# A streaming encoder layer: statistics of the last tiles taken at an earlier product, and the last product ended by column halves

## The chip, the cores and the metric

The kernel runs on one core of a Trainium2 chip. The metric is device time in microseconds, the median of several runs. Engines are named as in the profile: PE is TensorE (matmuls; PEld its weight loads), DVE is VectorE, ACT ScalarE, POOL GpSimd, SP SyncE, which issues most of the DMAs.

## The reference

One layer of a hybrid encoder in float32: a prompt of 2048 tokens and 128 tokens of eight streams, 17 tiles of 128 tokens with 1024 features. What matters here is the end of the layer, for each tile:

```python
f, conv_rows = conv_ffn(h, conv_prev, w_up, w_conv, b_conv, w_down)   # ends in (...) @ w_down, 2816 -> 1024
y = layer_norm(DEEPNORM_ALPHA * h + f, ln2_g, ln2_b)

def layer_norm(x, g, b):
    mu = jnp.mean(xf, axis=-1, keepdims=True)
    var = jnp.mean(jnp.square(xf - mu), axis=-1, keepdims=True)
    y = (xf - mu) * lax.rsqrt(var + LN_EPS) * g + b
```

Before it come the input projection, an mLSTM, a sliding-window attention, the output projection, a first layer norm and the up projection with its convolution and gate. The change touches none of that.

## The kernel before

The 17 tiles go through the feed-forward part in three blocks (`FBLOCKS`); the last block is tiles 12, 13, 14, 15 and 16. The down projection (`f_downs`) is the last stage. Each block's pairs of tiles and halves of `w_down` are multiplied by a Strassen-like scheme of seven products, numbered 1 to 7. The last block takes them in the order 1, 2, 4, 6, 5, 7, 3 (`DLAST`), so that "the second product" is number 2, "the sixth product" is the one numbered 6 and "the last product" is number 3. A product sums over 11 groups of 128 rows of `w_down`, taken two at a time in six units (`DUNITS`, the last with one group). A unit needs its weights and its activations split into a high and a low part: ACT rounds to the high part (L218), DVE subtracts (L219); tiles `uw` are split weights, `fu` split activations. Each group and tile costs three matmuls of 512 columns, high by high, high by low and low by high (L2090). The sums lie in eight banks of PSUM, one per tile and product, with the profile's names `dps`, `fup` and `fht`.

In the last block `ta` is tile 12 or 13 (for the product's column `p` 0 or 1) or tile 16 (`p` 2), `tb` tile 14 or 15. When a product is complete, `after` empties its bank: DVE adds it into the row block `yacc` of the tile (`add`, L2119 for the first contribution with the residual scaled by alpha, L2121 for the others). Product 2 completes the first 512 features of tiles 12, 13 and 16, product 3 the second 512. With product 3 each of these tiles is finished by `norm_last`: statistics of the two halves (`bn_stats`, L1564), their aggregate (L1565), the variance plus eps (L1566), GpSimd's power for the reciprocal root (L1567), two scalings of 512 columns by mean and gain (L1550), two by root and bias (L1552), each of these followed by its store. The last product takes tile 16, then 13, then 12. For tile 12 alone, `last_tile`, the first half's statistics are taken when product 2 is complete (L2102).

PE runs its instructions in the order in which the program writes them (`manual_schedule`). The instructions of the other engines are ordered by the tile framework's scheduler from dependencies and priorities; `add` runs at high priority. `tc.issue_after(i)` puts the instructions that its block writes behind instruction `i` on that instruction's engine. The framework also adds the semaphore waits between engines.

Of the kernel before, what the change touches and what calls it, by code (L numbers as in the profile page):

```python
# [8 lines left out]
F32 = mybir.dt.float32  # L9
F32R = mybir.dt.float32r  # L10
AF = mybir.ActivationFunctionType
ALU = mybir.AluOpType
AX = mybir.AxisListType

P = 128
# [32 lines left out]
HT = 2 * P  # L48
FBLOCKS = [[0, 1, 2, 3, 4, 5], [6, 7, 8, 9, 10, 11], [12, 13, 14, 15, 16]]
# [156 lines left out]
class Prog:  # L206
# [1338 lines left out]
    def norm_last(self, y, g, bb, dst, st):  # L1545

        nc, V = self.nc, self.nc.vector
        mv, s = self.stats(y, st)
        for c in (slice(0, 512), slice(512, 1024)):
            V.scalar_tensor_tensor(y[:, c], y[:, c], mv[:, 0:1], g[:, c], op0=ALU.subtract, op1=ALU.mult)  # L1550
        for c in (slice(0, 512), slice(512, 1024)):
            V.scalar_tensor_tensor(y[:, c], y[:, c], s[:, 0:1], bb[:, c], op0=ALU.mult, op1=ALU.add)  # L1552
            nc.sync.dma_start(dst[:, c], y[:, c])

    def stats(self, y, st=None):
        nc = self.nc
        V = nc.vector
        half = st is not None
        if not half:
            st = self.wp.tile([P, 2, 6], F32, name="lst", tag="lst", bufs=2)  # L1560
        mv = self.wp.tile([P, 2], F32, name="lmv", tag="lmv", bufs=2)
        s = self.wp.tile([P, 2], F32, name="lsc", tag="lsc", bufs=2)
        for i in range(half, 2):
            V.bn_stats(st[:, i], y[:, i * 512:(i + 1) * 512])  # L1564
        V.bn_aggr(mv, st)  # L1565
        V.tensor_scalar_add(s[:, 1:2], mv[:, 1:2], EPS)  # L1566
        nc.gpsimd.tensor_tensor(s[:, 0:1], s[:, 1:2], self.mhalf[:, 0:1], op=ALU.pow)  # L1567
        return mv, s
# [494 lines left out]
    def f_downs(self):  # L2063
        nc, a = self.nc, self.a
        V, S = nc.vector, nc.scalar
        mm = nc.tensor.matmul
        ln2 = []
        self.in_down = True
        for n in sorted(n for n in self.dq if n <= self.nt):
            for l in self.dq.pop(n):  # L2070
                self.d_load(*l)
        x = [self.fup.tile([P, 512], F32, name="fht", tag="fht", bufs=2) for _ in range(2)]
        banks = self.banks[0] + self.banks[1] + x


        role = {1: (0, 1, 2), 2: (0, 1, 2), 4: (3, 5, 0), 7: (3, 5, 2), 6: (6, 7, 4), 5: (6, 7, 4), 3: (6, 7, 4)}
        nb, nu = len(FBLOCKS), len(DUNITS)
        ys, ops = {}, {}
        last_tile = FBLOCKS[-1][0]
        st = self.wp.tile([P, 2, 6], F32, name="st", tag="st", bufs=1)  # L2080

        def product(s, p, units):
            ps = banks[role[s][2 if p == np_ else p]]
            c = slice(p * P, p * P + P)
            for u in units:
                wh, wl, fh, fl = ops[u]
                n = len(DUNITS[u])
                for k in range(n):
                    for i, (l, r) in enumerate(((fh, wh), (fh, wl), (fl, wh))):
                        mm(ps, l[:, k, c], r[:, k], start=s in (1, 4, 7) and u == 0 and k == 0 and i == 0,  # L2090
                           stop=u == nu - 1 and k == n - 1 and i == 2, skip_group_check=True)

        def after(s, p):
            ps = banks[role[s][2 if p == np_ else p]]
            ta, tb = (tiles[2 * np_], None) if p == np_ else (tiles[p], tiles[np_ + p])
            if s == 1:
                with self.tc.high_priority():
                    S.copy(banks[role[6][2 if p == np_ else p]], ps)
            elif s == 2:
                add(ta, 0, ps, True)  # L2100
                if ta == last_tile:
                    V.bn_stats(st[:, 0], ys[ta][:, :512])  # L2102
            elif s in (4, 6):
                add(tb, 0, ps, s == 4)
            elif s == 5 and tb is not None:
                add(tb, 1, ps, True)
            elif s == 7:
                add(tb, 0, ps, False)
                add(tb, 1, ps, False)
                pending.append(finish(tb, b, s))  # L2110
            elif s == 3:
                add(ta, 1, ps, True)
                pending.append(finish(ta, b, s))

        def add(t, half, ps, first):
            y = ys[t][:, half * 512:half * 512 + 512]
            with self.tc.high_priority():
                if first:
                    V.scalar_tensor_tensor(y, y, ALPHA, ps, op0=ALU.mult, op1=ALU.add)  # L2119
                else:  # L2120
                    V.tensor_add(y, y, ps)  # L2121

        def finish(t, b, step):
            if b == nb - 1 and step == 3:
                self.norm_last(ys[t], *ln2, a["y"][t], st if t == last_tile else None)
                return
            y, (g, bb) = ys[t], ln2
            mv, sc = self.stats(y)
            yield
            V.scalar_tensor_tensor(y, y, mv[:, 0:1], g, op0=ALU.subtract, op1=ALU.mult)  # L2130
            yield
            V.scalar_tensor_tensor(y, y, sc[:, 0:1], bb, op0=ALU.mult, op1=ALU.add)
            (nc.sync if b == nb - 1 else nc.gpsimd).dma_start(a["y"][t], y)

        pending = []

        def step():
            for f in pending[:2]:
                if next(f, self) is self:
                    pending.remove(f)  # L2140

        for g, (b, s, u) in enumerate(self.dseq):
            tiles = FBLOCKS[b]
            h, one = self.d_shape(b)
            np_ = h // P
            ts = [*tiles[:np_], *tiles[2 * np_:]] if s == 1 else tiles[np_:2 * np_] if s == 2 else []
            if 0 <= u - 2 < len(ts):
                t = ts[u - 2]
                ys[t] = self.f3.tile([P, D], F32, name="yacc", tag="yacc", bufs=6)
                nc.sync.dma_start(ys[t], self.zh[t])  # L2150
            if g == 3 * nu:
                for n in ("ln2_g", "ln2_b"):
                    t = self.fp.tile([P, D], F32, name="f_" + n, tag="hst", bufs=2)
                    nc.sync.dma_start(t, a[n].to_broadcast([P, D]))
                    ln2.append(t)
            ops[u] = *self.dw.pop((b, s, u)), *self.df.pop((b, s, u))
            if g == 0:
                for bank in x:
                    mm(bank, ops[0][2][:, 0, :P], ops[0][0][:, 0], start=True, stop=True, skip_group_check=True)
            cols = [*range(np_), *([np_] if one and s in (1, 2, 5, 3) else [])]  # L2160
            last = b == nb - 1 and s == DLAST[-1]
            if not last:
                for p in cols[::-1] if s == 7 else cols:
                    product(s, p, [u])
            elif u == 0:
                cols = cols[::-1]
                for p in cols:
                    product(s, p, [u])
            elif u == nu - 1:

                cols = cols[::-1]
                for p in cols:
                    product(s, p, range(1, nu))
                    after(s, p)
                    for _ in pending.pop():
                        pass

            if b < nb - 1:
                step()
            if u == nu - 1 and not last:  # L2180
                for p in cols[::-1] if s == 7 else cols:
                    after(s, p)
            while self.nw < min(g + 5, len(self.dseq)):
                self.d_weights()
            while self.nt < min(g + 6, len(self.dseq)):
                self.d_tokens()
            if b == nb - 1 and self.nw != len(self.dseq) - 1:
                with self.tc.issue_after(self.low):
                    step()
        while pending:  # L2190
            step()
# [15 lines left out]
```

## Time and profile before

| | us |
|---|---|
| median of 3 runs | 2295.34 (2293.25 to 2296.85) |
| the profiled execution | 2293.86 |
| its span, first to last instruction | 2292.1 |
| PE busy | 2273.5 |
| DVE busy | 1809.8 |
| ACT busy | 1272.4 |
| POOL busy | 278.7 |
| granted TensorE clock, mean | 0.999 |

A row of the timeline has the start, the time, the engine, the line, the operation, what it writes and reads, the shape, how many instructions are merged, and in brackets the engine's idle time before it and what ended that. A row of a group has the number of instructions behind the x, then their busy time and the mean of one in nanoseconds, then the idle time before them. A row of the waits has the waiting engine and what it waited for, the total, how often and the longest. The chain is followed back from the last instruction; the pieces of it are given in order of time.

### The profile page before, as it was taken

How to read it: one execution, taken by the hardware profiler on the slowest of the kernel's cores; microseconds unless marked ns; L12 is line 12 of the kernel's file. 1: busy time of each engine (PE TensorE's matmuls, PEld its weight loads, DVE VectorE, ACT ScalarE, POOL GpSimd, SP SyncE). 2: the span in 40 equal slices, each digit the busy share in tenths (PEclk: the TensorE clock that was granted, in tenths of full speed). 3: DMA queues.
4: the chain of work that ended last, by engine and by line, in shares of the span. 5: the costliest groups of instructions: out<-in, count | busy, mean ns of one | idle time of the engine just before them, and what ended most of it. 6: DMA issues, size and time to landing. Idle time of an engine off the chain costs nothing.

```text
span 2292.1 us, 39775 instructions
## 1 busy us (share of the span) xinstructions
PE 2273.5 (99%) x14293; PEld 2090.7 (91%) x14293; DVE 1809.8 (79%) x3068; ACT 1272.4 (56%) x2373; POOL 278.7 (12%) x509
## 2 busy tenths in 40 slices
PE   8999999999999999999999999999999999999998
PEld 8999999999878778999999999999999988888876
DVE  8777687777788879998778777778766786895987
ACT  5453476776766656555556555555555644444442
POOL 0001001000121110211112000013111200200200
PEclk9999999999999999999999999999999999999999
DMA  8989998898998867898778999988998786757752
GB/s 283 323 305 322 316 315 276 273 313 297 333 317 263 278 219 262 314 328 299 282 269 271 302 303 306 312 265 288 324 290 264 255 292 216 254 169 224 252 157 85
DMA packets 302133, 631.30 MB, mean 275 GB/s; under 512 B 47404, under 2 KB 140656, under 8 KB 301936
## 3 DMA queue, kind: packets, MB, share of 16 engines
q1 hardware_dynamic: 297264, 615.06, 79.2%
q0 software_dynamic: 3520, 10.56, 1.5%
q10 hardware_dynamic: 1152, 3.15, 0.4%
q8 instruction: 113, 1.85, 0.3%
q14 instruction: 84, 0.69, 0.1%
HBM read 457.02 MB, written 171.64 MB: 274 GB/s over the span
## 4 chain that ended last, share of the span: by engine, by line
PE 83%; DVE 3%; issue 1%; ACT 1%; DMA 1%; POOL 0%; SPq 0%; DVEq 0%; ACTq 0%; POOLq 0%
PE dps L1882 20%; PE fup L1882 20%; PE dps L713 8%; PE fup L2090 7%; PE dps L2090 7%; PE fht L2090 6%; PE dps L223 3%; PE dps L225 2%; PE dps L224 2%; PE ppo L1359 1%; PE ppt L1353 1%; PE psc L1314 1%; PE fht L1706 1%; PE pcu L1231 1%; PE dps L739 1%
## 5 line engine op out<-in xcount | busy, mean ns | idle before, releaser
L1882 PE MATMUL fup<-hh,uw 128*128 128x384 f32 (+1 forms) x1848 | 478.2, 328 | 0.0
L1882 PE MATMUL dps<-hh,uw 128*128 128x384 f32 (+1 forms) x1848 | 478.0, 328 | 0.0
L1882 PEld LDWEIGHTS fup<-hh,uw 128*128 128x128 f32 x1848 | 330.2, 188 | 0.0
L1882 PEld LDWEIGHTS dps<-hh,uw 128*128 128x128 f32 x1848 | 330.1, 188 | 0.0
L1882 PE MATMUL fup<-hl,uw 128*128 128x384 f32 (+1 forms) x924 | 302.9, 328 | 1.0 <-DVE hl L219 1.0
L1882 PE MATMUL dps<-hl,uw 128*128 128x384 f32 (+1 forms) x924 | 302.7, 328 | 0.0
L1940 DVE SCALAR_TENSOR_TENSOR cc<-u,cw,cc 128x768 f32<-128x768 f32 (+1 forms) x264 | 258.0, 978 | 39.3 <-ACT cc L1938 30.8
L713 PE MATMUL dps<-w,oh 128*128 128x256 f32 x1344 | 254.8, 285 | 0.1
L218 ACT CAST uw<-wraw 128x1024 fp32r<-128x1024 f32 x126 | 123.3, 978 | 228.2 <-PE dps L2090 122.2
L219 DVE TENSOR_TENSOR w<-wraw,w 128x1024 fp32r<-128x1024 f32 (+2 forms) x163 | 186.0, 1149 | 61.6 <-ACT w L218 58.6
L218 ACT CAST w<-wraw 128x1024 fp32r<-128x1024 f32 (+2 forms) x163 | 160.2, 992 | 113.8 <-PE dps L713 53.7
L713 PEld LDWEIGHTS dps<-w,oh 128*128 128x128 f32 x1344 | 210.9, 188 | 11.2 <-issue 8.1
L219 DVE TENSOR_TENSOR uw<-wraw,uw 128x1024 fp32r<-128x1024 f32 x126 | 142.2, 1129 | 61.2 <-ACT uw L218 61.2
L713 PE MATMUL dps<-w,ol 128*128 128x256 f32 x672 | 188.2, 280 | 0.0
L1882 PEld LDWEIGHTS fup<-hl,uw 128*128 128x128 f32 x924 | 173.7, 188 | 1.7 <-DVE hl L219 1.6
L1882 PEld LDWEIGHTS dps<-hl,uw 128*128 128x128 f32 x924 | 173.7, 188 | 0.0
L2090 PE MATMUL fup<-uw,fu 128*128 128x512 f32 x726 | 173.6, 396 | 0.0
L713 PE MATMUL dps<-oh,w 128*128 128x256 f32 x896 | 168.0, 283 | 3.9 <-DVE w L219 2.2
L2090 PEld LDWEIGHTS fup<-uw,fu 128*128 128x128 f32 x726 | 136.5, 188 | 32.7
L2090 PE MATMUL dps<-uw,fu 128*128 128x512 f32 x660 | 164.8, 396 | 0.0
L2090 PEld LDWEIGHTS dps<-uw,fu 128*128 128x128 f32 x660 | 124.1, 188 | 29.8
L713 PEld LDWEIGHTS dps<-oh,w 128*128 128x128 f32 x896 | 140.0, 188 | 10.1 <-issue 4.1
(320 smaller groups left out, 4567.6 us busy)
## 6 DMA issues: line engine op xcount, KB each, us to landing
uw<-zw SPq DMA_DIRECT2D x176, 512.0 KB, 5.0
zw<-uw SPq DMA_DIRECT2D x88, 512.0 KB, 3.3
w<-zws SPq DMA_DIRECT2D x72, 512.0 KB, 6.0
wv<-wup SPq DMA_DIRECT2D x66, 512.0 KB, 5.2
wraw<-wi SPq DMA_DIRECT2D x65, 512.0 KB, 5.2
wraw<-zt SPq DMA_DIRECT2D x60, 512.0 KB, 4.3
wraw<-wdn SPq DMA_DIRECT2D x45, 512.0 KB, 4.9
wraw<-wo SPq DMA_DIRECT2D x40, 512.0 KB, 5.1
```

The costliest lines, as they stand in the source:

```text
L218: nc.scalar.copy(hi, src)
L219: return nc.vector.tensor_sub(lo, src, hi.bitcast(F32)).ins
L223: mm(out, ah, bh, start=start, stop=False)
L224: mm(out, ah, bl, start=False, stop=False)
L225: mm(out, al, bh, start=False, stop=stop)
L713: mm(o, l, r, start=s in (1, 7) and c == k == i == 0, stop=k == 3 and i == 2, skip_group_check=True)
L739: mm(o, x, w, start=k == i == 0, stop=k == KD - 1 and i == 2, skip_group_check=True)
L1231: nc.tensor.matmul(ps[:, i], kw[:, h], v1[:, h], start=True, stop=True)
L1314: nc.tensor.matmul(ps[kvh][:, j, :nk], q[rs, j0 + j], k[rs, sel], start=i == 0, stop=i == 2)
L1882: mm(ps, l[:, k], r[:, k], start=s in (1, 7) and k == 0 and i == 0, stop=k == 3 and i == 2, skip_group_check=True)
L1940: V.scalar_tensor_tensor(c[:, v], u[:, i:i + n], w[i], c[:, v], op0=ALU.mult, op1=ALU.add)
L2090: mm(ps, l[:, k, c], r[:, k], start=s in (1, 4, 7) and u == 0 and k == 0 and i == 0, stop=u == nu - 1 and k == n - 1 and i == 2, skip_grou ...
```

## The change

Tiles 16, 13 and 12 each get a tag of their own for statistics, and when product 2 is complete all three have the statistics of their first half taken. Tile 12's are taken in two groups of 256 columns, so that its tile holds four groups. In the last product tiles 16 and 13 are done as before, with the statistics of their second half alone left to do. Tile 12's part of the product is written in two steps: units 1 to 3 over all 512 columns, then units 4 and 5 (three groups) over columns 0 to 255, then the same units over columns 256 to 511. After each half its add and its statistics follow, put behind tile 13's last scaling on DVE.

```diff
     def norm_last(self, y, g, bb, dst, st):
-        mv, s = self.stats(y, st)
+        mv, s = self.stats(y, st, True)
...
-            V.scalar_tensor_tensor(y[:, c], y[:, c], s[:, 0:1], bb[:, c], op0=ALU.mult, op1=ALU.add)
+            last = V.scalar_tensor_tensor(y[:, c], y[:, c], s[:, 0:1], bb[:, c], op0=ALU.mult, op1=ALU.add).ins
             nc.sync.dma_start(dst[:, c], y[:, c])
+        return last
+
+    def stat(self, st, y, half, *parts):
+        n = st.shape[1] // 2
+        w = 512 // n
+        for i in parts or range(n):
+            c = half * 512 + i * w
+            self.nc.vector.bn_stats(st[:, half * n + i], y[:, c:c + w])
...
-        for i in range(half, 2):
+        for i in range(2 if whole else half, 2):
             V.bn_stats(st[:, i], y[:, i * 512:(i + 1) * 512])
...
-        st = self.wp.tile([P, 2, 6], F32, name="st", tag="st", bufs=1)
+        early = (FBLOCKS[-1][-1], *FBLOCKS[-1][1::-1])
+        sts = {t: self.wp.tile([P, 4 if t == last_tile else 2, 6], F32, name="st", tag=f"st{i}", bufs=1) for i, t in enumerate(early)}
-        def product(s, p, units):
-            ps = banks[role[s][2 if p == np_ else p]]
+        def product(s, p, units, m=slice(0, 512)):
+            ps = banks[role[s][2 if p == np_ else p]][:, m]
...
-                        mm(ps, l[:, k, c], r[:, k], start=...)
+                        mm(ps, l[:, k, c], r[:, k, m], start=...)
...
                 add(ta, 0, ps, True)
-                if ta == last_tile:
-                    V.bn_stats(st[:, 0], ys[ta][:, :512])
+                if ta in sts:
+                    self.stat(sts[ta], ys[ta], 0)
...
-        def add(t, half, ps, first):
-            y = ys[t][:, half * 512:half * 512 + 512]
+        def add(t, half, ps, first, c=slice(0, 512)):
+            y, ps = ys[t][:, half * 512:half * 512 + 512][:, c], ps[:, c]
...
             if b == nb - 1 and step == 3:
-                self.norm_last(ys[t], *ln2, a["y"][t], st if t == last_tile else None)
+                if t != last_tile:
+                    self.stat(sts[t], ys[t], 1)
+                behind.append(self.norm_last(ys[t], *ln2, a["y"][t], sts[t]))
                 return
...
-                for p in cols:
+                for p in cols[:-1]:
                     product(s, p, range(1, nu))
                     after(s, p)
                     for _ in pending.pop():
                         pass
+                p = cols[-1]
+                product(s, p, range(1, nu - 2))
+                for i in range(2):
+                    m = slice(i * HT, i * HT + HT)
+                    product(s, p, range(nu - 2, nu), m)
+                    with self.tc.issue_after(behind[-1]):
+                        add(tiles[p], 1, banks[role[s][p]], True, m)
+                        self.stat(sts[tiles[p]], ys[tiles[p]], 1, i)
+                for _ in finish(tiles[p], b, s):
+                    pass
```

The built programs show what moves. The order on PE at the end of the program, with the semaphores that an instruction waits for; before (`fht` with x54 is tile 13's 27 matmuls and tile 12's 27):

```order
L2090 MATMUL dps<-uw,fu 128x512 x4
L2090 MATMUL dps<-uw,fu 128x512 [waits Activation_49]
L2090 MATMUL dps<-uw,fu 128x512 [waits DVE_49]
L2090 MATMUL dps<-uw,fu 128x512
L2090 MATMUL fht<-uw,fu 128x512 x54
```

and now:

```order
L2100 MATMUL dps<-uw,fu 128x512 [waits DVE_49]
L2100 MATMUL dps<-uw,fu 128x512
L2100 MATMUL fht<-uw,fu 128x512 x45
L2100 MATMUL fht<-uw,fu 128x256 x9
L2100 MATMUL fht<-uw,fu 128x256 [waits DVE_49]
L2100 MATMUL fht<-uw,fu 128x256 x8
```

Nine matmuls of tile 12 became eighteen of half the width, and the first of the second nine waits for DVE; the value it waits for is that of the add of columns 0 to 255, which is the second row of the piece of DVE after the change, below.

The order on DVE at the end of the program, from tile 13's scalings on; before (`lst` and `st` are statistics, `lmv` their aggregate, `lsc` the root's input and result):

```order
L1550 TENSOR_SCALAR yacc<-yacc,lmv,f_ln_g 128x512 x2
L1552 TENSOR_SCALAR yacc<-yacc,lsc,f_ln_b 128x512
L2119 TENSOR_SCALAR yacc<-yacc,fht 128x512
L1552 TENSOR_SCALAR yacc<-yacc,lsc,f_ln_b 128x512
L1564 BN_STATS st<-yacc 128x6
L1565 BN_AGGR lmv<-st 128x2
L1566 TENSOR_SCALAR lsc<-lmv 128x1
L1550 TENSOR_SCALAR yacc<-yacc,lmv,f_ln_g 128x512 x2
L1552 TENSOR_SCALAR yacc<-yacc,lsc,f_ln_b 128x512 x2
```

and now, from tile 13's last two scalings on:

```order
L1552 TENSOR_SCALAR yacc<-yacc,lsc,f_ln_b 128x512 x2
L2129 TENSOR_SCALAR yacc<-yacc,fht 128x256
L1562 BN_STATS st<-yacc 128x6
L2129 TENSOR_SCALAR yacc<-yacc,fht 128x256
L1562 BN_STATS st<-yacc 128x6
L1574 BN_AGGR lmv<-st 128x2
L1575 TENSOR_SCALAR lsc<-lmv 128x1
L1550 TENSOR_SCALAR yacc<-yacc,lmv,f_ln_g 128x512 x2
L1552 TENSOR_SCALAR yacc<-yacc,lsc,f_ln_b 128x512 x2
```

Both of tile 13's last scalings now stand ahead of tile 12's first add, and tile 12's add and statistics are two of each, in turn.

The order on DVE around the end of the sixth product, whose two adds (L2121, now L2131) empty the banks `fht` that the next product writes; before:

```order
L2121 TENSOR_TENSOR yacc<-yacc,fht 128x512
L219 TENSOR_TENSOR uw<-wraw,uw 128x1024
L2121 TENSOR_TENSOR yacc<-yacc,fht 128x512
L219 TENSOR_TENSOR fu<-r_23866,fu 128x2x256
L219 TENSOR_TENSOR fu<-r_23399,fu 128x2x128
```

and now:

```order
L219 TENSOR_TENSOR fu<-r_23868,fu 128x2x256
L219 TENSOR_TENSOR fu<-r_23401,fu 128x2x128
L2131 TENSOR_TENSOR yacc<-yacc,fht 128x512 x2
L219 TENSOR_TENSOR uw<-wraw,uw 128x1024
L219 TENSOR_TENSOR fu<-r_23868,fu 128x2x256
```

The weight split that stood between the two adds now stands behind both. At the end of the second product four BN_STATS rows stand where one stood (tile 12's two, and one each of tiles 13 and 16), and a subtraction of 256 columns (L2058, now L2067) moved from ahead of the sixth product's adds to behind them. The order on POOL and SP is unchanged, and that on ACT but for one activation split that moved by a unit.

More of the change, by code (lines that the diff above doesn't have):

```diff
@@ L1551, in norm_last, with stats @@
         for c in (slice(0, 512), slice(512, 1024)):
-            V.scalar_tensor_tensor(y[:, c], y[:, c], s[:, 0:1], bb[:, c], op0=ALU.mult, op1=ALU.add)
+            last = V.scalar_tensor_tensor(y[:, c], y[:, c], s[:, 0:1], bb[:, c], op0=ALU.mult, op1=ALU.add).ins
             nc.sync.dma_start(dst[:, c], y[:, c])
-    def stats(self, y, st=None):
+        return last
[5 more added lines that the diff above has]
+            self.nc.vector.bn_stats(st[:, half * n + i], y[:, c:c + w])
+    def stats(self, y, st=None, whole=False):
         nc = self.nc
@@ L2089, in product @@
                     for i, (l, r) in enumerate(((fh, wh), (fh, wl), (fl, wh))):
-                        mm(ps, l[:, k, c], r[:, k], start=s in (1, 4, 7) and u == 0 and k == 0 and i == 0,
+                        mm(ps, l[:, k, c], r[:, k, m], start=s in (1, 4, 7) and u == 0 and k == 0 and i == 0,
                            stop=u == nu - 1 and k == n - 1 and i == 2, skip_group_check=True)
@@ L2133, in finish @@
             (nc.sync if b == nb - 1 else nc.gpsimd).dma_start(a["y"][t], y)
-        pending = []
+        pending, behind = [], []
         def step():
```

## The prediction

> **What bounds the kernel now.** I read the page's busy times first, then TensorE's own waits, then the chain of work that ended last, and last the timeline of the two places where the programs differ. The busy times, the first and the last of the ten rows of TensorE's (PE's) waits, and the last piece of PE in the chain:
>
> ```profile
> PE 2273.5 (99%) x14293; PEld 2090.7 (91%) x14293; DVE 1809.8 (79%) x3068; ACT 1272.4 (56%) x2373; POOL 278.7 (12%) x509
> ```
>
> ```profile
> PE dps L713 <- DVE w L219: 2.2, 2, 1.4
> ...
> PE fht L2090 <- DVE yacc L2121: 0.2, 1, 0.2
> ```
>
> ```profile
> 2271.16 12.57 PE fht L2090 x54
> ```
>
> PE is busy for 99% of the span, and none of its waits names a DMA. So time can be won or lost in two ways only: PE is stopped somewhere, or the tail behind the last matmul changes. PE ends at 2271.16 + 12.57 = 2283.73, the span at 2292.1. What VectorE (DVE) does around that end:
>
> ```profile
> 2274.64 1.87 DVE L1564 BATCH_NORM_STATS2 lst<-yacc 128x6 f32<-128x512 f32 x3
> ...
> 2277.47 0.69 DVE L2119 SCALAR_TENSOR_TENSOR yacc<-yacc,fht 128x512 f32<-128x512 f32 x1
> 2278.08 0.74 DVE L1550 SCALAR_TENSOR_TENSOR yacc<-yacc,lmv,f_ln_g 128x512 f32<-128x512 f32 x1
> 2278.74 1.41 DVE L1552 SCALAR_TENSOR_TENSOR yacc<-yacc,lsc,f_ln_b 128x512 f32<-128x512 f32 x2
> 2280.07 0.68 DVE L1564 BATCH_NORM_STATS2 lst<-yacc 128x6 f32<-128x512 f32 x1
> 2280.78 0.21 DVE L1565 BATCH_NORM_AGGREGATE lmv<-lst 128x2 f32<-128x12 f32 x1
> 2281.03 0.15 DVE L1566 TENSOR_SCALAR lsc<-lmv 128x1 f32<-128x1 f32 x1
> 2281.10 1.41 DVE L1550 SCALAR_TENSOR_TENSOR yacc<-yacc,lmv,f_ln_g 128x512 f32<-128x512 f32 x2
> 2282.42 0.75 DVE L1552 SCALAR_TENSOR_TENSOR yacc<-yacc,lsc,f_ln_b 128x512 f32<-128x512 f32 x1
> 2283.75 0.69 DVE L2119 SCALAR_TENSOR_TENSOR yacc<-yacc,fht 128x512 f32<-128x512 f32 x1 [0.59 <-PE fht L2090]
> 2284.36 0.75 DVE L1552 SCALAR_TENSOR_TENSOR yacc<-yacc,lsc,f_ln_b 128x512 f32<-128x512 f32 x1
> 2285.02 0.69 DVE L1564 BATCH_NORM_STATS2 st<-yacc 128x6 f32<-128x512 f32 x1
> 2285.74 0.21 DVE L1565 BATCH_NORM_AGGREGATE lmv<-st 128x2 f32<-128x12 f32 x1
> ```
>
> After its last matmul DVE adds tile 12's product into the rows (2283.75), does one scaling that belongs to tile 13 (2284.36), then tile 12's statistics (2285.02) and their aggregate (2285.74). From the aggregate on both programs run the same instructions and the same last store. So the tail's change is the change in the moment at which tile 12's aggregate starts. The whole edit works on a few microseconds; 0.2% of 2295.34 is 4.6 us, about what a measurement of this kernel can tell from no change.
>
> **The change in the tail.** From start to start these rows give: an add 0.61 (2277.47 to 2278.08), two scalings 1.33 (2278.74 to 2280.07), statistics to their aggregate 0.71, aggregate to L1566 0.25, L1566 to the scaling 0.07. Of the three statistics at 2274.64 two go away, the first halves of tiles 16 and 13. In its new order DVE runs: tile 16's statistics 2274.64, aggregate 2275.35, scalings 2275.67 to 2277.00; tile 13's add as PE finishes it (27 of the 54 matmuls at 12.57/54 = 0.233), at 2277.47 as before; tile 16's last two scalings from 2278.08; tile 13's statistics 2279.41, aggregate 2280.12, L1566 2280.37, first two scalings 2280.44 to 2281.77. The last two wait for GpSimd's power:
>
> ```profile
> 2281.32 0.92 POOL L1567 TENSOR_TENSOR lsc<-lsc,mhalf 128x1 f32<-128x1 f32 x1 [3.46 <-DVE lsc L1566]
> ```
>
> It ends 1.21 behind the start of L1566 (2281.03 to 2282.24), now at 2281.58, in time. DVE is through with tile 13 at 2283.10.
>
> Now PE. Tile 12's last 27 matmuls become 18 of 512 columns, 9 of 256 on the left half of the bank and 9 of 256 on the right half. An early stage has 256 columns, and two DVE groups of the run's last 100 us show what width costs there:
>
> ```profile
> 60.27 0.39 PE L713 MATMUL dps<-oh,w 128*128 128x256 f32 x2
> ...
> 64.69 0.39 PE L713 MATMUL dps<-oh,w 128*128 128x256 f32 x2
> ```
>
> ```profile
> L219 DVE TENSOR_TENSOR fu<-r,fu 128x512 fp32r<-128x512 f32 x16 | 10.9, 683 | 0.0
> L219 DVE TENSOR_TENSOR fu<-r,fu 128x256 fp32r<-128x256 f32 x9 | 3.8, 418 | 0.1
> ```
>
> From 60.27 to 64.69 start 39 matmuls of 256 columns: 0.113 each, so two of them (0.227) cost no more than one of 512 (0.233), and the nine added instructions are free. The left half is done at 2277.44 + 18 x 0.233 + 9 x 0.113 = 2282.65. Its add, though, is queued behind tile 13's last scaling, so it runs at 2283.10. And PE's second group of nine waits for DVE in the new order: for that add, which reads the same bank. The trace has one such wait:
>
> ```profile
> 2220.87 0.69 DVE L2121 TENSOR_TENSOR yacc<-yacc,fht 128x512 f32<-128x512 f32 x1 [0.20 <-PE fht L2090]
> 2221.47 1.22 DVE L219 TENSOR_TENSOR uw<-wraw,uw 128x1024 fp32r<-128x1024 f32 x1
> 2222.61 0.68 DVE L2121 TENSOR_TENSOR yacc<-yacc,fht 128x512 f32<-128x512 f32 x1
> ```
>
> ```profile
> 2221.70 3.32 PE L2090 MATMUL fht<-uw,fu 128*128 128x512 f32 x12 [0.17 <-DVE yacc L2121]
> ```
>
> PE stood until the add on its bank was over (2220.87 + 0.69 = 2221.56) and began 0.14 later. The Trainium skill, "PSUM — Partial Sum Buffer", section "PSUM bank collisions raise a hardware error", says that TensorE writing and VectorE reading one bank collide even at different columns, and are to be kept apart by bank. By that rule the right half cannot overlap the add, and the row at 2221.70 agrees; were columns enough, the time would be the first rival's.
>
> A 256-wide add of this kind is not in the trace. By the two L219 rows 256 columns less save 0.265, so I take 0.42 for the add (0.69 less that) and 0.41 for the statistics, being nearest to these rows; the bounds are half the 512 row (0.34) and all of it (0.69). Then: left add 2283.10 to 2283.52; PE again at 2283.66; nine matmuls 1.02, and the last drains 0.28 in place of 0.11 (0.39 for a pair less 0.11), so 2284.85; right add 2284.87 to 2285.29; its statistics to 2285.72; aggregate at 2285.74, where it was. The tail's sum is 0.0. With the bounds for two adds and one statistics it runs from -0.2 to +0.8. The four-group aggregate in place of the two-group one I count as nothing (0.21 now, so at most 0.2 more). Without the halves, the early statistics alone would give 2283.75 + 0.69 + 0.02 + 0.69 + 0.02 = 2285.17, or -0.6: they gain, and the halves with their wait give it back.
>
> **The change at the second and sixth products.** After the second product's adds DVE gets four statistics for one: two of 512 columns more, and for tile 12 two of 256 in place of one of 512.
>
> ```profile
> 2191.53 0.68 DVE L2102 BATCH_NORM_STATS2 st<-yacc 128x6 f32<-128x512 f32 x1
> 2192.14 1.21 DVE L219 TENSOR_TENSOR uw<-wraw,uw 128x1024 fp32r<-128x1024 f32 x1
> ```
>
> ```profile
> 2190.61 15.54 PE L2090 MATMUL dps<-uw,fu 128*128 128x512 f32 x66
> ```
>
> One costs 0.61 (2191.53 to 2192.14); the increase is 2 x 0.61 + 0.05 = 1.27 us of DVE. The weight split behind it (2192.14 to 2193.35) is the fourth unit's of the product that PE begins at 2190.61, and PE needs it 36 matmuls later, at 2199.0. That cover of 5.6 us hides the 1.27; without it PE would wait 1.27.
>
> The scheduler also shifts DVE's rows up to the end of the sixth product. The chain there, and DVE's wait before the first add:
>
> ```profile
> 2221.70 1.64 PE fht L2090 x6
> ...
> 2223.34 1.68 PE fht L2090 x6
> ```
>
> ```profile
> DVE uw L219 <- ACT uw L218: 1.0, 2, 0.6
> ```
>
> Before, a weight split (2221.47) stands between the two adds, and PE's second six matmuls, whose bank the second add empties, start at 2223.34 and not 6 x 0.233 = 1.40 behind the first: 0.24 lost. Now the adds stand together, the second is over at 2222.25, and the 0.24 goes. Against it DVE reaches the first add with 1.27 more work, less a 256-wide subtraction moved behind (0.33), so 0.94; its idle time until there is 1.0 and 0.20 (the row at 2220.87), which holds that. With that cover gone PE would start 0.94 later. I take -0.2, with bounds -0.24 and +0.7.
>
> **Sum.** 0.0 - 0.2 = -0.2 us. The profiled execution took 2293.86 (its span 2292.1, 1.8 around it), so 2293.7 there. The median of the runs shown, 2295.34, lies 1.5 above it, so 2295.1. Both terms' bounds: -0.4 to +1.5.
>
> **The rivals.** First: the halves overlap, and PE doesn't wait for the left add. PE then ends at 2283.73 as before, DVE does the left add and its statistics from 2283.10 to 2283.95 and the right ones by 2284.83: the aggregate 0.9 earlier, with the other term 2294.2. For it speaks that the columns are disjoint, against it the wait in the order. Chance 0.10.
>
> Second: the pause costs more. The 256-wide steps cost nearly what 512 do, and DVE comes late to the sixth product's adds: +0.8 and +0.7, 2296.8. For it: the cover before the first add is thin (1.2 over 0.94); against it the 418 ns. Chance 0.18.
>
> Third, on the other side by more than 0.2%: two more tags for statistics lengthen a pool that was opened early, and in the built program the tiles of later pools on that side lie 160 bytes further in SBUF. About 169 MB of the kernel's transfers touch them. The queue's row, and the longest wait of a feeding engine for a DMA:
>
> ```profile
> q1 hardware_dynamic: 297264, 615.06, 79.2%
> ACT uw L218 <- DMA wv<-wup: 11.6, 5, 3.5
> ```
>
> If those transfers took 5% longer, that is 169/615 x 79.2% x 2292 x 5% = 25 us of queue time over the whole run. It decides where an engine that feeds PE already waits for a transfer; if a fifth reached PE, +5 us, 2300.3. Against it: PE's waits name no DMA, and a fifth of the queue's time is free. Chance 0.07. The Trainium skill, "DMA: Bandwidth & Descriptors", section "How a descriptor splits into AXI transactions", has a reason for it: a descriptor that starts off a 256-byte boundary fetches beats it does not use, by my estimate 5 on 128 for a 4 KiB row starting 160 bytes in. No run here shows it.
>
> The same shift could help instead, by as much: 2290.1, chance 0.05.
>
> **How the numbers follow.** My forecast has 0.60. Within 0.2% lie it and the first two rivals, 0.60 + 0.10 + 0.18 = 0.88; slower 0.07, faster 0.05. The likeliest gives 2295.1. The range goes from the first rival's 1.1 under the lowest run shown (2293.25, so 2292.1) to the upper bound over the highest (2296.85 + 1.5, so 2298.3) and leaves out the last two cases.
>
> **What would show it.** Right: a gap of about 1.0 us on PE before its last nine matmuls, ended by a 256-wide add at about 2283.1; tile 12's aggregate within 0.3 of 2285.74; the two adds of the sixth product side by side and one gap on PE there, not two. Wrong: no gap in the last product (first rival); 256-wide rows of 0.6, or PE stopped for over 0.5 at 2220 (second); DMA rows among PE's waits (third); or a span off by over 2 us with the tail as it was.

## The result, and the profile after

The changed kernel takes 2300.24 us (median of 10 runs, 2298.58 to 2301.26), beside 2294.02 (2293.01 to 2296.85) for the kernel before on the same chip: ratio 1.0025, 95% interval 1.0017 to 1.0033. It is slower by 0.25%, clear of noise, and lies above the predicted range. Its profiled execution took 2299.33 us, its span is 2297.6, 5.5 more than before.

The places that the change edits look as forecast. DVE's last rows in the timeline of the changed kernel, then PE's:

```profile
2287.09 1.41 DVE L1552 SCALAR_TENSOR_TENSOR yacc<-yacc,lsc,f_ln_b 128x512 f32<-128x512 f32 x2
2288.41 0.42 DVE L2129 SCALAR_TENSOR_TENSOR yacc<-yacc,fht 128x256 f32<-128x256 f32 x1
2288.86 0.43 DVE L1562 BATCH_NORM_STATS2 st<-yacc 128x6 f32<-128x256 f32 x1
2290.24 0.42 DVE L2129 SCALAR_TENSOR_TENSOR yacc<-yacc,fht 128x256 f32<-128x256 f32 x1 [0.95 <-PE fht L2100]
2290.70 0.43 DVE L1562 BATCH_NORM_STATS2 st<-yacc 128x6 f32<-128x256 f32 x1
2291.16 0.26 DVE L1574 BATCH_NORM_AGGREGATE lmv<-st 128x2 f32<-128x24 f32 x1
```

```profile
2276.30 11.73 PE L2100 MATMUL fht<-uw,fu 128*128 128x512 f32 x54
2288.89 1.32 PE L2100 MATMUL fht<-uw,fu 128*128 128x256 f32 x9 [0.86 <-DVE yacc L2129]
```

The row of 54 merges 45 matmuls of 512 columns and the first nine of 256; then PE stands 0.86 until the 256-wide add on its bank (2288.41 + 0.42 = 2288.83) is over. But everything comes 5.3 us late: the last product's group starts at 2276.30. In the timeline of the kernel before, the same group:

```profile
2270.99 12.72 PE L2090 MATMUL fht<-uw,fu 128*128 128x512 f32 x54
```

So 2276.30 - 2270.99 = 5.31 of the 5.5 us were lost before the tail. The page's busy times of the changed kernel, and its queue row:

```profile
PE 2279.9 (99%) x14302; PEld 2096.2 (91%) x14302; DVE 1810.0 (79%) x3071; ACT 1273.2 (55%) x2373; POOL 277.3 (12%) x509
```

```profile
q1 hardware_dynamic: 297264, 615.06, 79.4%
```

PE is busy 6.4 us longer with nine instructions more, and its waits, first and last two rows, name no DMA:

```profile
PE dps L713 <- DVE w L219: 2.1, 2, 1.3
...
PE pht L1187 <- ACT hn L1177: 0.2, 1, 0.2
PE fht L2100 <- DVE yacc L2131: 0.2, 1, 0.2
```

Where PE falls behind is found by setting the starts of its matmuls against those of the kernel before, one by one in program order: 0.2 us behind at the 600th, 2.3 at the 2000th, 4.0 at the 4400th, 4.5 at the 5600th (about 695 us), then 4.4 to 5.5 up to the tail. The loss builds up in the input projection, whose 256-column matmuls stand at L713 (`i_product`); the last of them starts at 615 us. Two of their groups, before and then after (the last number of the pair is the mean duration of one in ns):

```profile
L713 PE MATMUL dps<-oh,w 128*128 128x256 f32 x896 | 168.0, 283 | 3.9 <-DVE w L219 2.2 <-ACT mr L1164 1.0 <-ACT zev L779 0.7
L713 PE MATMUL dps<-ol,w 128*128 128x256 f32 x448 | 124.8, 279 | 0.0
```

```profile
L713 PE MATMUL dps<-oh,w 128*128 128x256 f32 x896 | 172.6, 286 | 3.4 <-DVE w L219 2.1 <-ACT zev L779 0.7 <-ACT mr L1164 0.6
L713 PE MATMUL dps<-ol,w 128*128 128x256 f32 x448 | 126.3, 282 | 0.0
```

The first tile behind the arrow is the moving operand, whose columns are streamed; the second is the stationary one, the loaded weights. One matmul is 3 ns longer, with no more idle time in front. Matmuls overlap (283 ns long, one started every 115 or so), so the price is the interval from start to start. Means over the trace (intervals over 150 ns left out): with `oh` or `ol` as the moving operand 115.5 ns before, 119.3 after; with `w` moving 117.3 before, 117.8 after. At one place it is plain to the eye. The prediction quoted 60.27 to 64.69 of the kernel before: 39 starts, 113 ns each. The changed kernel there, in its timeline:

```profile
60.14 0.41 PE L713 MATMUL dps<-oh,w 128*128 128x256 f32 x2
60.38 0.30 PE L713 MATMUL dps<-ol,w 128*128 128x256 f32 x1
...
64.77 0.43 PE L713 MATMUL dps<-oh,w 128*128 128x256 f32 x2
```

Thirty-six starts in 4.63 us, 129 ns each. This place is the extreme: in the whole trace 51 of the 1286 intervals with `oh` or `ol` moving lie between 130 and 136 ns, about half of them here, and none did before. Summed over the program, L713 gives 5.2 of the 5.28 us by which PE is late shortly before the end. The change touches neither these instructions nor their order: what differs is where their operands lie. In the built program `oh` and `ol` start on a multiple of 1024 bytes before, and 160 bytes behind one now, since the pool opened ahead of theirs holds two more statistics tiles; the weights `w` stay, 64 bytes off a multiple of 128.

### The profile page after: what moved, and what is told of

It reads as the page before. It is cut to its first block, busy times and chain, and to the rows that moved or that the text cites. A ratio compares the mean times of both kernels' runs of the same rounds, so it can differ in the third digit from the quotient of the medians.

```text
span 2297.6 us, 39794 instructions
## 1 busy us (share of the span) xinstructions
PE 2279.9 (99%) x14302; PEld 2096.2 (91%) x14302; DVE 1810.0 (79%) x3071; ACT 1273.2 (55%) x2373; POOL 277.3 (12%) x509
## 3 DMA queue, kind: packets, MB, share of 16 engines
q1 hardware_dynamic: 297264, 615.06, 79.4%
## 4 chain that ended last, share of the span: by engine, by line
PE 82%; DVE 4%; issue 1%; DMA 1%; ACT 1%; POOL 0%; DVEq 0%; SPq 0%; ACTq 0%; POOLq 0%
PE dps L1891 19%; PE fup L1891 19%; PE dps L713 8%; PE fup L2100 7%; PE dps L2100 7%; PE fht L2100 6%; PE dps L223 3%; PE dps L224 2%; PE dps L225 2%; PE ppo L1359 1%; PE ppt L1353 1%; PE psc L1314 1%; PE dps L739 1%; PE fht L1715 1%; DVE w L219 1%
## 5 line engine op out<-in xcount | busy, mean ns | idle before, releaser
L713 PE MATMUL dps<-w,oh 128*128 128x256 f32 x1344 | 255.9, 285 | 0.0
L713 PEld LDWEIGHTS dps<-w,oh 128*128 128x128 f32 x1344 | 211.1, 188 | 11.1 <-issue 8.1
L713 PE MATMUL dps<-w,ol 128*128 128x256 f32 x672 | 188.3, 280 | 0.0
L713 PE MATMUL dps<-oh,w 128*128 128x256 f32 x896 | 172.6, 286 | 3.4 <-DVE w L219 2.1
L1891 PEld LDWEIGHTS fup<-hl,uw 128*128 128x128 f32 x924 | 173.6, 188 | 1.6 <-DVE hl L219 1.5
L1891 PEld LDWEIGHTS dps<-hl,uw 128*128 128x128 f32 x924 | 173.6, 188 | 0.0
L713 PEld LDWEIGHTS dps<-oh,w 128*128 128x128 f32 x896 | 141.6, 188 | 9.5 <-issue 4.1
```

The costliest lines, as they stand in the source:

```text
L713: mm(o, l, r, start=s in (1, 7) and c == k == i == 0, stop=k == 3 and i == 2, skip_group_check=True)
L1891: mm(ps, l[:, k], r[:, k], start=s in (1, 7) and k == 0 and i == 0, stop=k == 3 and i == 2, skip_group_check=True)
```

## The experiments

Throughout, "place" is an operand's first byte in each partition modulo 128, and "distance" the difference of the two operands' places modulo 128 (32 and 96 are the same distance in the two directions and are both written 32).

**The change without the shift.** The two added statistics tiles go to the pool that is opened last, so that `oh`, `ol` and all other tiles of the early pools lie where they lay before.

```diff
-        sts = {t: self.wp.tile([P, 4 if t == last_tile else 2, 6], F32, name="st", tag=f"st{i}", bufs=1) for i, t in enumerate(early)}
+        sts = {t: (self.f3 if i else self.wp).tile([P, 4 if t == last_tile else 2, 6], F32, name="st", tag=f"st{i}", bufs=1) for i, t in enumerate(early)}
```

> The changed kernel, but the statistics tiles of 13 and 12 come from the pool that is opened last, so that every other pool lies where it lay before (only r4 and yacc of the last pool move by 160 bytes). Address theory (the 6 us come from the tiles of the early pools lying 160 bytes further): 2293.8, that is -0.2 against before, and the input projection's 256-column matmuls with oh or ol as moving operand at 115.5 ns each as before, not 119.4. Order theory (the added and moved instructions cost it): 2300, as the changed kernel.

Measured: 2293.91 us (2292.84 to 2296.07), ratio 0.9998 (0.9988 to 1.0008); 115.6 ns. With its edits of order all in, the change costs nothing; the shift is the whole loss.

**The kernel before, shifted.** Unused bytes in its one statistics tile push the later pools by 160, 32, 64, 128 and 256 bytes; no instruction differs. For 32:

```diff
-        st = self.wp.tile([P, 2, 6], F32, name="st", tag="st", bufs=1)
+        st = self.wp.tile([P, 24], F32, name="st", tag="st", bufs=1)[:, :12].rearrange("p (a b) -> p a b", b=6)
```

> The kernel before, with its statistics tile lengthened by 160 bytes that nothing uses, so that the later pools lie as in the changed kernel. Address theory: +5.5 us (2299.5), first matmul of the down projection about 5 us later, all of it lost before 650 us. Order theory: 2294.0, no change.

> The kernel before with 32 bytes of padding. Theory that an operand off a 64-byte boundary slows PE: +5.5 us as with 160. Theory that transfers off a 256-byte boundary are slower: also slower, by the same. Tells whether 160 is special.

> The kernel before with 64 bytes of padding: on a 64-byte boundary, off a 256-byte one. Theory of 64 bytes at PE: 2294.0, no change, oh/ol matmuls at 115.5 ns. Theory of 256 bytes at the DMAs: slower, about +5 us, with longer landings.

> The kernel before, with 128 unused bytes in the statistics tile, so that every tile of the pools opened later on that side lies 128 bytes further in SBUF; no instruction differs. The address theory (a 256-column matmul takes longer when its moving tile does not start on a boundary) comes in two forms. If the boundary is of 128 bytes: 2294 us, L713 with oh or ol moving 115.5 ns from start to start as in the kernel before. If it is of 256 bytes or more: 2300 us, and 119 ns. The rival, that any length added to this pool disturbs something else than the matmuls' reads, expects 2300 us with 115.5 ns.

> The kernel before, with 256 unused bytes in the statistics tile; no instruction differs. A boundary of 128 or of 256 bytes: 2294 us and 115.5 ns from start to start of the L713 matmuls with oh or ol moving. A boundary of 512 or 1024 bytes, or a cost of any shift whatever: 2300 us and 119 ns.

Measured: 2300.58 (ratio 1.0028, 1.0017 to 1.0038), 2301.21 (1.0030, 1.0020 to 1.0041), 2302.00 (1.0034, 1.0021 to 1.0047), 2295.58 (1.0006, 0.9996 to 1.0015) and 2294.53 us (1.0001, 0.9991 to 1.0010); the matmuls with `oh` or `ol` moving took 119.0, 119.3, 119.1, 115.2 and 115.4 ns. So 160 unused bytes alone reproduce the loss; 64 cost as much as 32, where the run's expectation had named 2294.0 for a boundary of 64, and 128 are free. By then a boundary of 128 bytes for the moving operand looked like the cause.

**Only `oh` and `ol` put back.** In the changed kernel, unused bytes ahead of them put these tiles on a multiple of 256; the input rows, tables and later pools stay shifted by 160 or by more.

```diff
+        if q == 4:
+            return self.xp.tile([P, 4 * HT + 24], F32, name="xr", tag="xr4", bufs=1)[:, :4 * HT].rearrange("p (a b) -> p a b", b=HT)
...
-        r = self.mp.tile([P, nt, 3, 32], F32, name="ropet", tag=f"ropet{nt}", bufs=nt)
+        r = self.mp.tile([P, nt * 96 + 8 * (nt == 2)], F32, name="ropet", tag=f"ropet{nt}", bufs=nt)[:, :nt * 96].rearrange("p (t a b) -> p t a b", a=3, b=32)
```

> The changed kernel with its longer pool, in which only the tiles oh and ol are put back on a boundary of 256 bytes by unused bytes in front of them; xr, the tables and the tiles of later pools stay off it (by 160 bytes, some by others). If the matmuls of L713 that read oh and ol as the moving operand carry the cost: 115.5 ns from start to start, 2294 us (at most 2295). If other tiles that were shifted carry it (weights, input rows, transfers): 2300 us still, whatever oh and ol do.

Measured: 2295.22 us (2293.59 to 2295.63), ratio 1.0003 (0.9994 to 1.0012), 115.4 ns. The two tiles carry the cost; all that was shifted besides them, transfers included, costs nothing that these runs can tell.

**The weights on the boundary too.** If a boundary mattered for whichever operand moves, `w`, which lies 64 bytes off one, should gain. A wider constant moves the weights by 64 bytes, and 64 more in the statistics tile keep `oh` and `ol` on a multiple of 128. The second kernel has the same over the kernel of the last experiment below, the early statistics without the halves.

```diff
-        self.mhalf = cp.tile([P, 8], F32, name="mhalf")
+        self.mhalf = cp.tile([P, 24], F32, name="mhalf")
...
-        st = self.wp.tile([P, 2, 6], F32, name="st", tag="st", bufs=1)
+        st = self.wp.tile([P, 28], F32, name="st", tag="st", bufs=1)[:, :12].rearrange("p (a b) -> p a b", b=6)
```

> The kernel before, with 64 unused bytes among the constants and 64 more in the statistics tile: the weight tiles w (64 bytes off a 128-byte boundary in the kernel before) lie on one, and oh and ol still do. If the cost belongs to any 256-column matmul whose moving tile starts off a 128-byte boundary, those of L713 with w moving (117.3 ns from start to start, 2016 of them) go to about 115.4 as those with oh moving, which is 2016 x 1.9 = 3.8 us: 2290.3 us, ratio 0.9983. If the effect is particular to oh and ol (or to the shift of the later pools): 117.3 still, 2294.1 us.

> The early statistics without the column halves, and the weight tiles on a 128-byte boundary as well. If both gains are real and independent, 0.5 us from the tail and 3.8 us from the matmuls: 2289.8 us, ratio 0.9981, faster than both kernels. If the boundary theory fails for w: 2293.6 us, no change that the times can tell.

Measured: 2300.16 (ratio 1.0025, 1.0016 to 1.0035) and 2299.81 us (1.0025, 1.0016 to 1.0034): six slower where four faster was expected. Both kinds became slow, 119.0 ns with `oh` or `ol` moving, which had not left their place, and 118.7 with `w` moving. Groups of the first of the two kernels:

```profile
L713 PE MATMUL dps<-w,oh 128*128 128x256 f32 x1344 | 257.5, 286 | 0.0
...
L713 PE MATMUL dps<-oh,w 128*128 128x256 f32 x896 | 172.4, 286 | 3.5 <-DVE w L219 2.1 <-ACT mr L1164 0.7 <-ACT zev L779 0.7
```

The boundary theory falls. These figures are those of the kernel with 64 unused bytes (119.1 and 118.8), where both operands lie 64 bytes off a boundary and not on it; what the two share is the distance, 0. In the kernel before it is 64.

**The distance kept, both places moved.** The wider constant alone moves the weights and all behind them, by 64 bytes (24 numbers, as above) or by 32 (16).

```diff
-        self.mhalf = cp.tile([P, 8], F32, name="mhalf")
+        self.mhalf = cp.tile([P, 16], F32, name="mhalf")
```

> The kernel before, with 64 unused bytes among the constants only: weights w, and the tiles oh and ol behind them, all lie 64 bytes further (w on a 128-byte boundary, oh and ol 64 bytes off it), so that the distance between the two operands of a matmul stays what it is in the kernel before, an odd multiple of 64 bytes. If the distance modulo 128 decides (64 cheap; 0 and 32 dear): 115.5 ns from start to start of the L713 matmuls with oh or ol moving, 117.3 with w moving, 2294 us. If the place of each operand decides: oh 64 bytes off a boundary as in the kernel with 64 bytes in the statistics tile, 119 ns, 2300 to 2302 us.

> The kernel before, with 32 unused bytes among the constants only: w, oh and ol all lie 32 bytes further, none of them on a multiple of 64, the distance kept. If the distance decides: 115.5 and 117.3 ns, 2294 us. If a boundary of 64 or 128 bytes has a part in it as well: 119 ns with oh moving, 2300 us.

Measured: 2293.53 us (ratio 0.9997, 0.9987 to 1.0007) and 2288.83 (2288.10 to 2291.14; 0.9977, 0.9968 to 0.9987). With `oh` or `ol` moving 115.1 and 114.9 ns, with `w` moving 117.0 in both. Groups of the kernel with 64:

```profile
L713 PE MATMUL dps<-w,oh 128*128 128x256 f32 x1344 | 254.2, 284 | 0.2 <-ACT dps L807 0.2
...
L713 PE MATMUL dps<-oh,w 128*128 128x256 f32 x896 | 167.4, 282 | 3.9 <-DVE w L219 2.3 <-ACT mr L1164 0.9 <-ACT zev L779 0.7
```

`oh` now lies at the very address that it had in the slow kernel with 64 unused bytes, and is fast. For L713 the distance decides and not either operand's place, as far as these means tell; all kernels together (they ran on several chips, on which the kernel before took 2293.8 to 2294.4 us):

| distance | kernels | `oh`, `ol` moving, ns | `w` moving, ns | us |
|---|---|---|---|---|
| 64 | before; without the shift; 128; 256; `oh` put back; early statistics (below); both by 64 | 115.1 to 115.6 | 117.0 to 117.3 | 2293.5 to 2295.6 |
| 64 | both by 32; both by 96 (two kernels, below) | 114.9 to 115.2 | 117.0 to 117.1 | 2288.5 to 2289.1 |
| 32 | the change; 160; 32 | 119.0 to 119.3 | 117.8 to 117.9 | 2300.2 to 2301.2 |
| 0 | 64; weights on the boundary (two kernels) | 119.0 to 119.1 | 118.7 to 118.8 | 2299.8 to 2302.0 |

The 5 us that 32 bytes won were not expected. Matmul by matmul, 4.4 of the 5.7 us by which PE is earlier at the end come from the down product, L2090, whose 512-column matmuls start 230.8 ns apart instead of 233.0. One of its groups before, and with the 32 bytes:

```profile
L2090 PE MATMUL fup<-uw,fu 128*128 128x512 f32 x726 | 173.6, 396 | 0.0
```

```profile
L2090 PE MATMUL fup<-uw,fu 128*128 128x512 f32 x726 | 172.0, 393 | 0.0
```

The activations `fu` lie in a pool on the other side of SBUF and did not move. The weights `uw` of 1587 of the 1980 matmuls lie in the pool of `w`, those of the other 393 in a pool behind it. Their distance was 32 for all, and is now 0 for the 1587 and 64 for the 393. (The expectation of the 96-byte run counts 1583 of the 1587.)

**The same with 96 bytes**, in the kernel before (32 numbers in the constant) and in the next experiment's kernel: the distance at L2090 becomes 64 for the 1587 and 0 for the others.

> The kernel before, with 96 unused bytes among the constants: the distance of w to oh and ol stays 64 modulo 128. In the last stage's down product (L2090, 512 columns) the distance of the weights uw to the activations fu becomes 64 modulo 128 for four matmuls in five (32 or 96 in the kernel before, 0 with 32 unused bytes) and 0 for the fifth. If the distance decides there too, and by the same steps as in the run with 32 bytes (233 ns at 32 or 96, 231.0 at 0, 229.7 at 64): 229.7 ns for four in five, 1976 matmuls together 1583 x 3.2 + 393 x 2.4 = 6.0 us less, and with the 1.3 us that the run with 32 bytes had gained ahead of them 2287.1 us. If the place of uw decides (32 modulo 128 against 96): 231 to 233 ns, 2289 to 2293 us.

> The early statistics without the column halves, with the 96 unused bytes: if both add up, 0.5 us under the run above, 2286.6 us, ratio 0.997, faster than both kernels. If only the weights' place in the run with 32 bytes was lucky: 2289 to 2293 us.

Measured: 2289.05 us (2287.57 to 2290.63; ratio 0.9979, 0.9970 to 0.9988) and 2288.53 (2287.45 to 2290.03; 0.9976, 0.9967 to 0.9985), both faster than the kernel before and the changed one, and no better than 32 bytes as far as these runs tell; 2287.1 and 2286.6 were expected. The mean at L2090 in the first is 231.1 ns, so the gain came again; but it did not grow, as the 229.7 expected for distance 64 would have made it: the 1587 took 230.8 at distance 64 and the other 393 232.3 at 0, where with 32 bytes they took 231.0 at 0 and 229.7 at 64.

**The early statistics without the halves**, nothing shifted: tile 12 ends with 512-column matmuls and one add.

```diff
-                for p in cols[:-1]:
+                for p in cols:
...
-                p = cols[-1]
-                product(s, p, range(1, nu - 2))
-                for i in range(2):
...
-                        add(tiles[p], 1, banks[role[s][p]], True, m)
-                        self.stat(sts[tiles[p]], ys[tiles[p]], 1, i)
...
```

> The changed kernel without the column halves: the three first-half statistics are made early, the last product ends with 512-column matmuls and one add, and the two added statistics tiles lie in the pool opened last, so nothing is shifted. By the sum on record the early statistics alone bring tile 12's aggregate 0.6 us earlier (about 2285.1 in the trace, against 2285.64 with the halves and without the shift), and the halves with their wait on PE give that back; 2293.4 us, which the times alone cannot tell from 2294. The rival, that the halves cost nothing or gain, expects the aggregate at 2285.6 or later.

Measured: 2293.78 us (2291.85 to 2294.72), ratio 0.9997 (0.9987 to 1.0007). In its timeline PE and DVE have:

```profile
2272.27 12.72 PE L2100 MATMUL fht<-uw,fu 128*128 128x512 f32 x54
```

```profile
2285.03 0.69 DVE L2129 SCALAR_TENSOR_TENSOR yacc<-yacc,fht 128x512 f32<-128x512 f32 x1 [0.59 <-PE fht L2100]
2285.76 0.69 DVE L1562 BATCH_NORM_STATS2 st<-yacc 128x6 f32<-128x512 f32 x1
2286.48 0.21 DVE L1574 BATCH_NORM_AGGREGATE lmv<-st 128x2 f32<-128x12 f32 x1
```

In this execution PE reached the last product 1.28 us later than before (2272.27 against 2270.99), so the aggregate's time is taken from the start of that product: 14.21 here. In the kernel without the shift:

```profile
2270.80 11.69 PE L2100 MATMUL fht<-uw,fu 128*128 128x512 f32 x54
2283.36 1.33 PE L2100 MATMUL fht<-uw,fu 128*128 128x256 f32 x9 [0.87 <-DVE yacc L2129]
```

```profile
2285.64 0.26 DVE L1574 BATCH_NORM_AGGREGATE lmv<-st 128x2 f32<-128x24 f32 x1
```

That is 2285.64 - 2270.80 = 14.84 with the halves, and it was 2285.74 - 2270.99 = 14.75 before. The early statistics win 0.54 and the halves with PE's pause lose 0.63, in one trace of each kernel; the times (2293.78 and 2293.91 us) cannot tell these apart.

## Why the prediction was wrong

**The sum left out the term that decided.** The step that failed is the sentence that time can be won or lost "in two ways only: PE is stopped somewhere, or the tail behind the last matmul changes". There is a third: PE is not stopped, but its matmuls follow one another more slowly. What came true is the prediction's last sign of being wrong, a span off by over 2 us (5.5) with the tail as it was. The sum had two terms, -0.2 us, both at places that the change edits; the third, for the shift of later pools, stood only as a rival with chance 0.07. That chance was the mistake. What it rested on, that PE waits for no DMA and the queue has room, speaks against slow transfers alone. The same tiles are read by 3360 matmuls on the engine that is busy 99% of the time, and the prediction never asked whether these could run slower. A third of a per cent there, 0.4 ns on each, already costs 1.3 us; it was 3.8 ns on the 1344 that have `oh` or `ol` moving and 0.5 ns on the 2016 with `w` moving. Matmul by matmul, waits included, the first gave 4.1 us and the second 1.1. The base was off too, by less: 2295.34 came from three runs, and ten gave 2294.02.

**The third rival was right in its place and in its 5 us, and wrong in its mechanism.** No row of PE's waits names a DMA. The queue's share went from 79.2% of 2292.1 to 79.4% of 2297.6, 9 us of queue time where the rival had 25, and ACT's wait that the prediction quoted has hardly changed (12.4 us in all against 11.6, the longest 3.2 against 3.5):

```profile
ACT uw L218 <- DMA wv<-wup: 12.4, 6, 3.2
```

That row's tile `wv` lies besides in the pool of `w`, which did not move; ACT's waits for `xr`, a tile that did move, came to 3.5 us after 4.1. The kernel with `oh` and `ol` alone put back leaves the other tiles off a boundary of 256 bytes and is not slow; nor are the kernels in which the weights and all behind them lie 32, 64 or 96 bytes further. So what the Trainium skill says in "DMA: Bandwidth & Descriptors", section "How a descriptor splits into AXI transactions", of beats fetched in vain off a 256-byte boundary did not show as time here. That the rival's 2300.3 lies next to the 2300.24 measured is chance: its "a fifth reaches PE" was free.

**The tail: right.** Forecast 0.0 (-0.2 to +0.8); from the start of the last product to the aggregate 14.86 (2291.16 - 2276.30) against 14.75, +0.1, and +0.1 again without the shift, where the aggregate came at 2285.64, inside the 0.3 of 2285.74 that the prediction named. The steps: add 0.42 (forecast 0.42), statistics 0.43 (0.41), PE's pause 0.86 (about 1.0), the four-group aggregate 0.26 against 0.21, and the early statistics by themselves -0.54 (-0.6).

**The wait of the second half: right, so the first rival falls.** The Trainium skill, "PSUM — Partial Sum Buffer", section "PSUM bank collisions raise a hardware error", has the two halves of one bank collide. The 0.86 on PE's row agrees, but it is a wait that the built program asks for; no run here lets the two overlap.

**The sixth product: right.** Its two adds stand side by side, with one gap on PE. DVE's rows of the changed kernel and PE's:

```profile
2226.39 1.39 DVE L2131 TENSOR_TENSOR yacc<-yacc,fht 128x512 f32<-128x512 f32 x2 [0.17 <-PE fht L2100]
2227.70 1.22 DVE L219 TENSOR_TENSOR uw<-wraw,uw 128x1024 fp32r<-128x1024 f32 x1
```

```profile
2227.22 3.03 PE L2100 MATMUL fht<-uw,fu 128*128 128x512 f32 x12 [0.17 <-DVE yacc L2131]
```

PE's lateness fell from 5.51 to 5.29 us over these products, -0.2 as forecast, and DVE was in time for the first add: it still idled 0.17 ahead of it. The second rival falls on both of its legs.

**What stays open.** Why the distance counts: weight loads (PEld, busy for 91% of the span) and matmuls (PE, 99%) overlap, so two streams read SBUF at once, and at distance 64 they may meet less often; that is argued, not shown. Every run that moves `w` moves its whole pool, raw weights included, so for L713 it is not shown either that `w` itself, and not a neighbour that is being written, is the partner of `oh`; the up projection (last section) speaks for the operands themselves. For L2090 a rule by distance alone is not shown: every kernel whose 1587 main matmuls had a distance of 0 or 64 took 230.8 to 231.1 ns in the mean, those with 32 took 232.5 to 233.3, but in the changed kernel the other 393, at distance 64, took 233.8. More than that: in the kernels with 32 unused bytes in the statistics tile and with 32 among the constants, both operands of these 393 lie at the very same addresses, and they took 233.1 and 229.7 ns. So there something besides their own two addresses has a part: the tiles of the weights' pool, which lie 32 bytes apart in the two kernels, or the matmuls ahead of them. No run separates these. That the 0.5 us of the early statistics adds to the gain of the 96 bytes fits the two medians (2288.53 and 2289.05), but is below what these runs can tell.

## What to carry to other kernels

A tile added to a pool is also a change to the address of every tile of the pools opened behind it; on a kernel bound by PE, compare the two operands' addresses of the large matmul groups before and after, modulo 128 bytes, and price the shift on PE as well as on the queues. To test an edit by itself, put its new tiles in the pool that is opened last, or fill the old pool up to the next 128 bytes (128 and 256 unused bytes cost nothing here). Trying a few offsets between the operands' pools costs one unused line of bytes, and here won more (5 us) than the edit it was found with could have (0.5).

## What the runs showed of the hardware

In the mean, a 256-column matmul of L713 is started every 115 ns when its operands lie 64 bytes apart modulo 128, and every 119 ns at 0 or 32, with `oh` or `ol` moving; with `w` moving it is 117.0 to 117.3 at 64, 117.8 to 117.9 at 32 and 118.7 to 118.8 at 0. The up projection (L1882 in the kernel before) has several distances in one and the same trace, and its 384-column matmuls show the same order, smaller: in each of the 16 traces those at 64 have the shortest mean, 173.6 to 174.3 ns, against 174.3 to 175.1 at 0 and 174.8 to 175.6 at 32, where these occur. It also holds for the weights that lie outside the pool of `w`: 173.7, 174.7 and 175.3 over all traces. At 320 columns it is 146.5 at 64 and 146.7 otherwise, over all traces. Durations on DVE did not change with the shift: 0.69 us for the 512-wide add, 0.42 for the 256-wide, in kernels with and without it.
